# Memory keys, sample attention and the hand-over to the output projection: first weight splits two steps later, the keys' inverse root on GpSimd with later transposes, output-projection weights and the attention mix fetched ahead and split in two column ranges

## The chip, the cores and the metric

The kernel runs on one core of one Trainium2 chip. The metric is the device time of one execution in microseconds (us); lower is better. Times "before" are three timed executions and one profiled execution. The profile was taken on that core.

## What is computed

The reference is one layer of a streaming encoder for a prompt of 1024 rows and a sample of 64 rows that share the weights. Cut to what matters here:

```python
h  = rms_norm(x, g_norm1)
q, k, v, f = split(h @ w_in)                # two kinds of heads, A and B, 8 each, width 64
mix = concat(attend_A(...), attend_B(...))  # 1088 rows (1024 prompt, 64 sample) x 1024
x  = x + mix @ w_o                          # the output projection
kv = rms_norm(mem, g_mem) @ w_mkv           # 256 memory rows, 2048 columns
mk = rms_norm(kv[:, :1024] in 4 heads of 256, g_mk)   # keys;  mv = kv[:, 1024:]
x  = x + mem_attend(rms_norm(x, g_norm2), mk, mv) @ w_mo
x  = x + conv_ffn(rms_norm(x, g_norm3))
```

Every float32 product is made of two parts, "hi" (rounded) and "lo" (what the rounding left), so one product is three matmuls: hi·hi, lo·hi, hi·lo. A **split** is therefore two instructions: a copy on ScalarE that makes hi, and a subtraction on VectorE or GpSimd that makes lo.

## The kernel before, in words

The program is one long straight run of instructions. The code states the work in an order, and a planner then fixes the order of each engine's queue from dependencies and its own estimate of durations; at run time each queue is strictly in order. The stages are: the input projection with prompt attention woven in; the memory keys and values, woven with the attention of the 64 sample rows; the output projection; memory attention; the feed-forward part. All DMAs are issued from the queue of SyncE (SP), also in order.

The change lies between the end of prompt attention and the start of the output projection.

**End of prompt attention** (helpers at L460 to L566). For a head, two score groups are multiplied into one PSUM pair "S" (L499), GpSimd adds the forget bias into a row buffer `s` (L485, L486), VectorE takes the row maximum (L502), ScalarE the exponential (L504), ScalarE or GpSimd scales (L509, L507), TensorE transposes 128x128 blocks into `PT` (L539), which are split (L540, L541) and multiplied with the values into `O` (L554). ScalarE copies half of `O` (`otmp`, L563), VectorE adds the halves (`mix`, L564), SP stores the result to DRAM (`mixd`).

**Memory stage.** L876 to L881 load the memory's first weights and input, split the input (`mhi`, `mlo`, L265 and L266) and, with `split_wm(0, 0)` and `split_wm(0, 1)`, half of the first weights (`mwhi`, `mwlo`, L668 and L669). Then the last four steps of prompt attention follow (`LEFT`, L882); fifteen memory pieces are woven into the last of them. There are 16 **units** (n, t): eight column blocks n of 256, of which n = 0 to 3 are keys and 4 to 7 values, times two row tiles t. A unit is 4 pieces of 6 matmuls into a bank of `pj` (L679); `pj` has two banks, so a unit takes the bank of the unit two before it. `mem_end` finishes a unit. For a key ScalarE squares and sums (`sq`, L695), VectorE adds a constant (L696), `rsq` (L71 to L80) makes the inverse root with a logarithm and an exponential on ScalarE and three small steps on VectorE, and VectorE scales out of the bank (`kv`, L698). `mem_turn` transposes the key on TensorE (L710). It stands in the third piece of the next unit.

**Sample attention.** Eight samples (pairs of heads) go through `load`, `prep`, `splitk`, `score`, `splitv`, `turn`, `sum`, `out` (L717 to L849), each a step behind the other; `PER` says how many memory pieces are woven into each step. Cached keys come through `kraw` buffers, of which there are three. The result goes into `smix`.

**Hand-over.** When no memory piece is left, `open_left` (L962) gives up the memory's SBUF, opens the pool of the projection's streamed weights (`Stream`, L902, splits at L919 and L920), and splits the mix: eight rows k of 1024 columns, each one copy on ScalarE (L979) and one subtraction on VectorE (L980), from `mraw` buffers. In the last step the first of two products is woven in, `first` = output rows m = 0, column ranges 0 and 1; the projection's `ORDER` (L1087) starts with them. L1022 and L1023 add the sample's 64 columns.

## Time and profile before

| what | value |
|---|---|
| median of 3 timed runs | 1781.4 us (1781.03 to 1784.44) |
| profiled execution, its own time | 1788.58 us |
| span of the profile | 1786.6 us |
| TensorE busy | 1717.5 us, 96% of the span |
| VectorE, ScalarE, GpSimd busy | 68%, 53%, 36% |
| prompt attention ends, first memory matmul | 598.69 us |
| last memory matmul starts | 699.47 us |
| first projection matmul on the mix | 710.55 us |

How to read the profile lines: in the timeline each row is a start (us), a duration (us), the engine, the line of the kernel, the operation, and out<-in; "x3" says that three like instructions were merged; the bracket gives the idle time of that engine just before and what ended it. In the table by windows each engine has its busy time and the number of instructions in a stretch; the three last columns are the granted TensorE clock (1.00 is full speed), the busy share of the DMA engines and GB/s. A row of the groups has the count, the busy time in all, and the mean duration in ns. PE is TensorE, DVE VectorE, ACT ScalarE, POOL GpSimd.

### The profile page before, as it was taken

What the parts mean: (1) busy time and instruction counts of PE and PEld (TensorE: products, weight loads), DVE (VectorE), ACT (ScalarE), POOL (GpSimd) and SP (SyncE); (2) the same over time, 40 slices, a digit from 0 to 9 for tenths busy, and PEclk for the clock granted to TensorE, in tenths of its full rate; (3) what the DMA queues carried; (4) which work ended last, traced back from release to release, by engine and by line L of the source; (5) the groups of instructions that cost most, each with busy time, mean ns of one, the idle gap of its engine ahead of it and who ended that gap; (6) DMA issues with size and microseconds to landing.
All of it is one profiled execution on the core that took longest, in us unless ns stands there. A gap on an engine that the chain in (4) does not pass through costs nothing.

```text
span 1786.6 us, 33930 instructions
## 1 busy us (share of the span) xinstructions
PE 1717.5 (96%) x12432; PEld 1668.3 (93%) x12432; DVE 1210.5 (68%) x2643; ACT 941.2 (53%) x2058; POOL 647.3 (36%) x931
## 2 busy tenths in 40 slices
PE   7898999999998898999999999999999999999999
PEld 6888999999997777999999999999999999999999
DVE  5768667677677686433444369877777777649986
ACT  6756667677677577433555456434333333434432
POOL 4556667778777443453443612100000000000000
PEclk8999999999999999999999999999999999999999
DMA  7322222122112777541111563222222222693332
GB/s 251 91 62 64 60 77 78 49 74 76 51 56 83 216 252 219 165 143 56 54 54 60 151 214 104 79 75 77 79 85 85 85 73 73 216 346 130 118 104 88
DMA packets 134391, 199.87 MB, mean 112 GB/s; under 512 B 20984, under 2 KB 74360, under 8 KB 134224
## 3 DMA queue, kind: packets, MB, share of 16 engines
q1 hardware_dynamic: 134224, 197.70, 35.0%
q8 instruction: 98, 1.61, 0.4%
q14 instruction: 69, 0.57, 0.1%
HBM read 155.35 MB, written 45.44 MB: 112 GB/s over the span
## 4 chain that ended last, share of the span: by engine, by line
PE 46%; DVE 4%; issue 2%; ACT 1%; POOL 1%; DMA 1%; SPq 0%; DVEq 0%; ACTq 0%; POOLq 0%
PE W L1449 24%; PE W L1773 11%; PE pj L937 7%; PE S L1192 1%; PE tq L1228 1%; PE O L1228 1%; POOL lo L920 1%; DVE f L1314 0%; PE PT L1215 0%; DMA f<-x2d 0%; DVE lo L920 0%; DMA h<-ad 0%; PE O L1192 0%; ACT hi L1313 0%; DVE qhi L1301 0%
## 5 line engine op out<-in xcount | busy, mean ns | idle before, releaser
L299 PE MATMUL pj<-whi,xhi 128*128 128x384 f32 (+1 forms) x512 | 195.8, 382 | 2.7 <-DVE flog L314 1.6
L299 PE MATMUL pj<-wlo,xhi 128*128 128x384 f32 (+1 forms) x512 | 177.0, 346 | 4.3 <-POOL wlo L123 4.3
L299 PE MATMUL pj<-whi,xlo 128*128 128x384 f32 (+1 forms) x512 | 175.9, 344 | 0.7 <-DVE xlo L131 0.7
L1555 POOL COPY s<-gp 128x2 f32<-128x2 f32 x22 | 15.8, 720 | 335.8 <-DVE gp L1554 335.8
L1449 PE MATMUL W<-h,hi 128*128 128x272 f32 x704 | 134.4, 288 | 1.4 <-ACT qlo L1585 1.4
L504 ACT ACTIVATE s<-s,mx 128x640 f32<-128x640 f32 (+7 forms) x128 | 94.4, 737 | 77.4 <-DVE mx L502 76.5
L1773 PE MATMUL W<-f,hi 128*128 128x272 f32 x672 | 127.1, 287 | 0.1
L541 DVE TENSOR_TENSOR ptl<-PT,pth 128x512 fp32r<-128x512 f32 (+2 forms) x192 | 99.4, 522 | 37.5 <-ACT pth L540 35.3
L1449 PEld LDWEIGHTS W<-h,hi 128*128 128x128 f32 x704 | 110.8, 188 | 1.6 <-ACT qlo L1585 1.6
L540 ACT CAST pth<-PT 128x512 fp32r<-128x512 f32 (+2 forms) x192 | 84.7, 449 | 41.7 <-PE PT L539 39.9
L1773 PEld LDWEIGHTS W<-f,hi 128*128 128x128 f32 x672 | 105.3, 188 | 0.4 <-DVE f L1520 0.4
L299 PEld LDWEIGHTS pj<-wlo,xhi 128*128 128x128 f32 x512 | 99.5, 194 | 5.9 <-POOL wlo L123 5.9
L299 PEld LDWEIGHTS pj<-whi,xhi 128*128 128x128 f32 x512 | 99.4, 194 | 4.3 <-DVE flog L314 1.9
L1449 PE MATMUL W<-h,lo 128*128 128x272 f32 x352 | 101.8, 289 | 0.0
L299 PEld LDWEIGHTS pj<-whi,xlo 128*128 128x128 f32 x512 | 98.3, 192 | 1.4 <-DVE xlo L131 1.2
L1773 PE MATMUL W<-f,lo 128*128 128x272 f32 x336 | 96.7, 288 | 0.0
L539 PE MATMUL PT<-ident,s 128*128 128x128 f32 x528 | 89.9, 277 | 6.9 <-DVE ptl L541 5.4
L1313 ACT CAST hi<-raw 128x512 fp32r<-128x512 f32 x68 | 42.2, 621 | 98.6 <-PE W L1449 59.2
L499 PE MATMUL S<-kh,q 128*128 128x256 f32 (+1 forms) x304 | 77.8, 281 | 13.5 <-DVE mx L502 13.5
L937 PE MATMUL pj<-a,hi 128*128 128x384 f32 (+1 forms) x352 | 89.3, 337 | 0.2 <-DMA mraw<-mixd 0.2
L507 POOL TENSOR_SCALAR s<-s,ssum 128x640 f32<-128x640 f32 (+6 forms) x96 | 70.8, 738 | 47.9 <-DVE ssum L505 34.3
L554 PE MATMUL O<-pth,v 128*128 128x256 f32 (+1 forms) x304 | 76.5, 277 | 8.5 <-DVE mix L564 7.7
(538 smaller groups left out, 6037.6 us busy)
## 6 DMA issues: line engine op xcount, KB each, us to landing
raw<-in_w_down_dram SPq DMA_DIRECT2D x45, 256.0 KB, 2.8
wraw<-in_w_dram SPq DMA_DIRECT2D x56, 192.0 KB, 2.5
raw<-in_w_up_dram SPq DMA_DIRECT2D x41, 256.0 KB, 2.8
h<-ad SPq DMA_DIRECT2D x32, 272.0 KB, 5.5
mwraw<-in_w_mkv_dram SPq DMA_DIRECT2D x16, 512.0 KB, 6.1
raw<-in_w_mo_dram SPq DMA_DIRECT2D x32, 256.0 KB, 3.2
kvraw<-in_w_down_dram SPq DMA_DIRECT2D x32, 256.0 KB, 3.0
ad<-t SPq DMA_DIRECT2D x22, 272.0 KB, 2.2
```

The lines of the kernel that those rows point to most:

```text
L299: pe.matmul(pj[:, :nw], x2[a][:, k, t * P:(t + 1) * P], wt[k][b][:, :nw], start=n == 0, stop=n == 3 * KT - 1)
L499: pe.matmul(sp[:, a:a + (k1 - k0) * P], q, kk[:, h, src], start=m == 0, stop=m == 1)
L504: act.activation(s[:, :n], s[:, :n], ACT.Exp, bias=mx, scale=-1.0, accum_out=sm)
L507: pool.tensor_scalar(s[:, :n], s[:, :n], sm, 1.0, op0=ALU.mult, op1=ALU.mult)
L539: pe.transpose(pt[:, b - ch[0]], self.s[j][:, (b - w0) * P:(b - w0 + 1) * P], ident)
L540: act.copy(hi[:, f:f + n, j], pt[:, f:f + n])
L541: dve.tensor_tensor(lo[:, f:f + n, j], pt[:, f:f + n], f32(hi[:, f:f + n, j]), op=ALU.subtract)
L554: pe.matmul(op[:, cols], groups[p, b // 2].v[:, b % 2, h].rearrange("p a d -> p (a d)"), pt[:, x, cols], start=b == self.full[0] and m == ...
L937: pe.matmul(out()[:, :cn], w[a][:, k % 4], x[b][k][:, c0:c0 + cn], start=k == 0 and n == 0, stop=k == KT - 1 and n == 2)
L1313: act.copy(hi, t)
L1449: pe.matmul(w[:, z, :Q], a(p, j), rights[j][b][:, z * Q:z * Q + Q], start=fresh and begin and j == 0 and x == 0, stop=final and end and j ...
L1773: pe.matmul(ws[m][:, z, :Q], la[p][:, m * P:(m + 1) * P], ra[b][:, z * Q:z * Q + Q], start=first and y == 0 and what in opening, stop=fina ...
```

## The change

Four things are edited.

1. `split_wm(0, 0)` and `split_wm(0, 1)` stand two steps of prompt attention later.
2. A key's constant and inverse root are two GpSimd instructions (an add, and a power of -0.5 with `mhalf`) in place of one VectorE step, two ScalarE steps and three VectorE steps. The key's transpose stands in the second piece of the unit after the next, and `kv` has three buffers in place of two.
3. The pool of the streamed weights and of `x0` lies beneath the memory's pool, so it is open from the start of the stage: the first loads are stated at sample step 4, the first four splits at steps 5 and 6. The first six mix rows are loaded at steps 4 to 6, the last two in `open_left`, all into buffers of the samples' pool: five `mraw`, and the `kraw` buffers, which the samples' keys also use. `sqd` has one buffer in place of two.
4. The mix is split in two column ranges, 0 to 384 and 384 to 1024, in 16 pieces; the first two products are both of column range 0 (m = 0 and m = 1), and `ORDER` starts with these.

```diff
-STAGE, MIXES = 4, 8
+MIXES = 8
+MIXED = {4: ("mraw",) * 2, 5: ("mraw",) * 2, 6: ("mraw", "kraw")}
+WEIGHTS = 5
...
-    left = ExitStack()
+    left, late_left = ExitStack(), ExitStack()
+    wr = late_left.enter_context(tc.tile_pool(name="wr", bufs=1, side="left"))
+    early_x = late_left.enter_context(tc.tile_pool(name="x0", bufs=1, side="left")).tile([P, 384], F32, name="x0")
...
-            dve.tensor_scalar(ms, ms, emem[:, t:t + 1], None, op0=ALU.add)
-            rsq(mp, ms, r, 1)
+            pool.tensor_scalar(ms, ms, emem[:, t:t + 1], 1.0, op0=ALU.add, op1=ALU.mult)
+            pool.tensor_tensor(r, ms, mhalf[:, 0:1], op=ALU.pow)
...
-                if c == 2 and u:
-                    mem_turn(*units[u - 1])
+                if c == 1 and u > 1:
+                    mem_turn(*units[u - 2])
...
-    split_wm(0, 0)
-    split_wm(0, 1)
-    for n in LEFT:
+    for x, n in enumerate(LEFT):
+        if x == 2:
+            split_wm(0, 0)
+            split_wm(0, 1)
         step(n, substeps())
...
-    first = [Product(2 * m, mixr, c, c == 2) for m, c in ((0, 0), (0, 1))]
+    first = [Product(2 * m, mixr, c, c == 2) for m, c in ((0, 0), (1, 0))]
...
+        def split_mix(k, c):
+            hi, lo = (mixr[z][k][:, c] for z in range(2))
+            act.copy(hi, mraws[k][:, c])
+            dve.tensor_tensor(lo, mraws[k][:, c], f32(hi), op=ALU.subtract)
+
+        for k in range(6, KT):
+            load_mix("kraw")
+
+        return ha, [lambda k=k, c=c: split_mix(k, c) for c in (slice(0, first_), rest_) for k in range(KT)]
...
+        for tag in MIXED.get(x, ()):
+            load_mix(tag)
+        if x == WEIGHTS - 1:
+            stream.fetch()
+            nc.sync.dma_start(early_x, i["xT"][0, :, 0:384])
...
+        if WEIGHTS <= x < WEIGHTS + 2:
+            subs += [lambda n=n: stream.upto(n) for n in (2 * (x - WEIGHTS) + 1, 2 * (x - WEIGHTS) + 2)]
```

What the planner makes of it is seen in the queues. All five are the same before and after up to the end of prompt attention and again from the third product of the projection on.

**ScalarE, at the end of prompt attention.** Before, two splits of the memory's weights (`mwhi`) stand ahead of the copy of `O` (`otmp`):

```order
L265 ACTIVATE mhi<-s,gcol 128x256 x3
L668 CAST mwhi<-mwraw 128x512 x2
L563 COPY otmp<-O 64x256
L540 CAST pth<-PT 128x4x128 x2
L668 CAST mwhi<-mwraw 128x512 x2
L265 ACTIVATE mhi<-s,gcol 128x256 x4
L504 ACTIVATE s,ssum<-s,mx 128x896
L540 CAST pth<-PT 128x128
L509 ACTIVATE s<-s,ssum 128x896
L540 CAST pth<-PT 128x2x128
L504 ACTIVATE s,ssum<-s,mx 128x1024
```

Now the same stretch reads (`hi<-raw` is a split of the projection's first streamed weights):

```order
L267 ACTIVATE mhi<-s,gcol 128x256 x3
L565 COPY otmp<-O 64x256
L542 CAST pth<-PT 128x4x128 x2
L672 CAST mwhi<-mwraw 128x512 x2
L542 CAST pth<-PT 128x128
L672 CAST mwhi<-mwraw 128x512
L542 CAST pth<-PT 128x2x128
L267 ACTIVATE mhi<-s,gcol 128x256 x4
L506 ACTIVATE s,ssum<-s,mx 128x896
L565 COPY otmp<-O 64x256
L672 CAST mwhi<-mwraw 128x512
L929 CAST hi<-raw 128x512
```

The copy of `O` stands ahead of the weights, and two of the weights' copies have gone behind the next exponential. All four of the projection's stated first splits have come up to the end of prompt attention: the first is the last row shown, the others stand up to 14 rows later, two of them behind the last exponential.

**GpSimd, at the first two key units.** Before, between the last scaled scores and the first sample's small steps (`s<-s,stok` is the sample's forget bias, `mwlo` the low part of a memory weight):

```order
L762 TENSOR_SCALAR s<-s,stok 128x1088
L669 TENSOR_TENSOR mwlo<-mwraw,mwhi 128x512
L892 MEMSET sq_9094 128x128
L892 MEMSET sq_9095 128x128
L765 AFFINE_SELECT s<-s 64x64 x2
```

Now, with the roots (`mms` is the squared sum, `mr` the inverse root) of the first and the second unit:

```order
L700 TENSOR_SCALAR mms<-mms,emem 128x1
L701 TENSOR_TENSOR mr<-mms,mhalf 128x1
L766 TENSOR_SCALAR s<-s,stok 128x1088
L673 TENSOR_TENSOR mwlo<-mwraw,mwhi 128x512
L896 MEMSET sq_9077 128x128
L896 MEMSET sq_9078 128x128
L769 AFFINE_SELECT s<-s 64x64 x2
L673 TENSOR_TENSOR mwlo<-mwraw,mwhi 128x512
L700 TENSOR_SCALAR mms<-mms,emem 128x1
L701 TENSOR_TENSOR mr<-mms,mhalf 128x1
```

The second unit's root stands behind a sample's bias, two weight splits and four small steps.

**TensorE, at the hand-over.** Before, from the end of the seventh sample's sum (`su` is a sample's finished result, `s` its weights, `a` the mix):

```order
L835 MATMUL O<-svh,ptl 128x256
L847 MATMUL PT<-ident,su 64x128
L822 MATMUL PT<-ident,s 128x128 x4
L822 MATMUL PT<-ident,s 64x128
L937 MATMUL pj<-a_10467,hi 128x384
```

Now, from the last rows of the eighth sample's sum (`vc` and `svh` are the high parts of cached and new values):

```order
L839 MATMUL O<-vc,ptl 128x256
L839 MATMUL O<-svh,pth 128x256
L839 MATMUL O<-svh,ptl 128x256
L949 MATMUL pj<-a_10458,hi 128x384 x2
L949 MATMUL pj<-a_10466,hi 128x384
```

The first product on the mix stood ahead of the eighth sample's sum and now stands behind it. Between the last memory matmul and this product the queue also holds the seventh sample's transposes and sum and the eighth's queries and scores, with no memory matmul among them.

More of the change, by code (lines that the diff above doesn't have):

```diff
@@ L725, in load @@
             p, n = self.p, self.ctx + S
-            self.qd = mq.tile([S, 4, P], F32, name="sqd", bufs=2)
+            self.qd = mq.tile([S, 4, P], F32, name="sqd", bufs=1)
             nc.sync.dma_start(self.qd.rearrange("t h d -> t (h d)"), sqk[p])
@@ L869, in hybrid_step @@
             line.append(piece)
-    line.append(lambda: mem_turn(*units[-1]))
     def step(n, subs):
@@ L892, in hybrid_step, with load_mix @@
         pool.memset(f32(zq[x][:, 1:3]), 0.0)
+    mraws = []
+    def load_mix(tag="mraw"):
+        k = len(mraws)
+        mraws.append(mq.tile([P, T], F32, name=tag, bufs={"mraw": 5, "kraw": 3}[tag]))
+        nc.sync.dma_start(mraws[k], mixd[k])
     samples = [Sample(p) for p in SAMPLES]
@@ L928, in done @@
             self.upto(j + 5)
+    stream = Stream(wr)
     def gemm(out, j, x, chunk, end):
@@ L962, in open_left @@
     def open_left():
[L963 removed]
         left.close()
[L965 to L967 removed]
         ha = mixes.enter_context(tc.tile_pool(name="ha", bufs=1, side="left"))
[L969 removed]
         mixr.extend(parts(ha, "a"))
[L971 to L990 removed]
+        first_, rest_ = CHUNKS[0][1], slice(CHUNKS[0][1], T)
+        def split_mix(k, c):
[5 more added lines that the diff above has]
+        return ha, [lambda k=k, c=c: split_mix(k, c) for c in (slice(0, first_), rest_) for k in range(KT)]
     old, mixes_todo, ha = [], [], None
@@ L1008, in hybrid_step @@
         del line[:PER[x]]
-        if ha and not mixes_todo:
-            stream.upto(4)
-            if todo:
-                main = todo.pop(0).pieces
+        if WEIGHTS <= x < WEIGHTS + 2:
+            subs += [lambda n=n: stream.upto(n) for n in (2 * (x - WEIGHTS) + 1, 2 * (x - WEIGHTS) + 2)]
+        if ha and len(mixes_todo) <= KT:
+            main = todo.pop(0).pieces
         subs += mixes_todo[:MIXES]
@@ L1085, in project @@
                 deferred.append((4, lambda c=c: after(c, acc[c])))
-    ORDER = [(0, 0), (0, 1), (1, 0), (0, 2), (1, 1), (1, 2)] + [(m, c) for m in range(2, 8) for c in range(3)]
+    ORDER = [(0, 0), (1, 0), (0, 1), (0, 2), (1, 1), (1, 2)] + [(m, c) for m in range(2, 8) for c in range(3)]
     e2 = hb.tile([P, 9], F32, name="e2")
```

27 lines of the change are left out of this document (3 added, 24 removed).

## The prediction

> **What bounds the kernel now.** I read the head of the page, then the busy times and the granted clock in windows around the change, then TensorE's waits, then the timeline.
>
> ```profile
> span 1786.6 us, 33930 instructions
> PE 1717.5 (96%) x12432; PEld 1668.3 (93%) x12432; DVE 1210.5 (68%) x2643; ACT 941.2 (53%) x2058; POOL 647.3 (36%) x931
> ```
>
> TensorE is busy for 96% of the span, so an edit can only win what TensorE idles, or runs at a reduced clock, where the change acts.
>
> ```profile
> 574.00:575.00 1.00, 0.00 (x0) 0.00 (x0) 0.00 (x0) 0.69 (x2) 1.00 (x4) 0.50 1.00 384
> 584.00:585.00 1.00, 0.67 (x5) 0.46 (x4) 1.00 (x1) 0.12 (x1) 0.93 (x2) 0.91 1.03 418
> 707.00:708.00 1.00, 0.00 (x0) 0.00 (x0) 0.91 (x1) 0.95 (x3) 0.00 (x0) 0.53 0.94 303
> 717.00:718.00 1.00, 1.00 (x8) 1.00 (x8) 1.00 (x3) 1.00 (x2) 0.00 (x0) 0.85 0.79 260
> 725.00:735.00 10.00, 10.00 (x63) 10.00 (x62) 3.26 (x6) 5.15 (x10) 4.72 (x4) 1.00 0.62 183
> ```
>
> The columns are the stretch, then PE, PEld, DVE, ACT, POOL busy, then the granted clock. The queues agree up to the end of prompt attention and again from the third projection product, and from 725 TensorE has no gap. So everything is decided between 571 and 725. In it lie two windows at half clock, of some 10 us each (574 to 584, 707 to 717), each begun in a gap of TensorE, and between them small waits:
>
> ```profile
> PE PT L710 <- DVE kv L698: 3.5, 4, 1.3
> PE pj L679 <- POOL mwlo L669: 2.0, 3, 1.0
> ```
>
> These are TensorE's two largest waits from 598 to 701 (total us, times, longest): the key that must be transposed, and the low part of a memory weight.
>
> **A. The weights' splits two steps later.**
>
> ```profile
> 574.31 1.14 ACT L668 CAST mwhi<-mwraw 128x512 fp32r<-128x512 f32 x2 [1.24 <-DMA mwraw<-in_w_mkv_dram]
> ...
> 575.47 0.37 ACT L563 COPY otmp<-O 64x256 f32<-64x256 f32 x1
> ...
> 575.48 3.00 DVE L669 TENSOR_TENSOR mwlo<-mwraw,mwhi 128x512 fp32r<-128x512 f32 x1 [1.89 <-ACT mwhi L668]
> ...
> 575.69 1.01 POOL L485 TENSOR_SCALAR s<-bias,ctok 128x896 f32<-128x896 f32 x1
> ...
> 577.89 0.74 POOL L486 TENSOR_SCALAR_AFFINE_SELECT s<-s 128x128 f32<-128x128 f32 x1
> ...
> 578.51 0.42 DVE L564 TENSOR_TENSOR mix<-O,otmp 64x256 f32<-64x256 f32 x1
> ...
> 578.85 1.07 DVE L502 CUSTOM_DVE_ANT_0 s<-S,s 128x896 f32<-128x896 f32 x1
> ...
> 579.07 0.55 PE L554 MATMUL O<-pth,v 128*128 128x256 f32 x1 [7.69 <-DVE mix L564]
> ...
> 598.69 0.28 PE L679 MATMUL pj<-mwhi,mhi 128*128 128x256 f32 x1
> ```
>
> TensorE stands 7.69 us for `mix`, which stands behind the subtraction of 3.00, and its `otmp` behind two copies that waited for a DMA. With the splits later, `otmp` follows the `mhi` rows that end at 573.06 (574.31 − 1.24), `mix` comes at about 573.6, and TensorE restarts near 574.1, 5.0 earlier. All of that does not come through. The next link is the first row maximum (578.85). It needs GpSimd's bias, which ends at 576.70 (575.69 + 1.01), and its selection, up to 0.74 more, so it can start near 577.1, 1.7 earlier; the four maxima then follow each other through one pair of banks. ScalarE also gets the four stream splits here, at 0.57 each (half of 1.14), two behind the last exponential. I take +1.6 for the gain at the first memory matmul (598.69 to about 597.0), between 0 (the stream splits eat it) and 5.0.
>
> **B. The root on GpSimd, the transpose a unit later, first four keys.**
>
> ```profile
> 602.69 0.39 ACT L695 ACTIVATE sq<-pj 128x256 f32<-128x256 f32 x1 [1.82 <-PE pj L679]
> ...
> 606.05 0.48 DVE L698 SCALAR_TENSOR_TENSOR kv<-pj,mr,gmk 128x256 f32<-128x256 f32 x1
> ...
> 606.68 0.41 PE L710 MATMUL PT<-ident,kv 128*128 128x128 f32 x2 [1.27 <-DVE kv L698]
> ...
> 610.98 0.41 PE L710 MATMUL PT<-ident,kv 128*128 128x128 f32 x2 [1.01 <-DVE kv L698]
> ...
> 615.34 0.41 PE L710 MATMUL PT<-ident,kv 128*128 128x128 f32 x2 [0.86 <-DVE kv L698]
> ...
> 724.23 0.51 PE L937 MATMUL pj<-a,hi 128*128 128x384 f32 x2
> ...
> 724.76 0.51 PE L937 MATMUL PT<-a,hi 128*128 128x384 f32 x2
> ```
>
> The nearest rows for the new instructions are GpSimd's groups in the prompt's norms (four columns where the new ones have one; the mean ns of one is behind the comma):
>
> ```profile
> L250 POOL TENSOR_TENSOR r<-m,mhalf 128x4 f32<-128x4 f32 x32 | 32.7, 1021 | 31.0 <-DVE m L249 30.2
> ...
> L244 POOL TENSOR_SCALAR m<-m,eps 128x4 f32<-128x4 f32 x32 | 9.3, 290 | 60.2 <-DVE m L241 60.2
> ```
>
> From `sq` to the end of `kv` is now 3.84 (602.69 to 606.53). The new chain is `sq` 0.39 and its read-out 0.2, the add 0.29, the power 1.02, `kv` 0.48, with handoffs about 2.7. The transpose a unit later has a whole unit in hand: 24 matmuls of 256 columns, by the three of 384 columns in 0.53 (724.23 to 724.76) 0.177 × 2/3 = 0.12 each, 2.9. So the 3.5 of key waits go. What is late next is the bank: with two banks of `pj`, unit u + 2 waits for `kv` of unit u, and GpSimd's queue decides that.
>
> ```profile
> 601.29 1.18 POOL L762 TENSOR_SCALAR s<-s,stok 128x1088 f32<-128x1088 f32 x1 [0.52 <-DMA s<-negs]
> ...
> 604.24 1.30 POOL L669 TENSOR_TENSOR mwlo<-mwraw,mwhi 128x512 fp32r<-128x512 f32 x1 [1.77 <-ACT mwhi L668]
> ...
> 605.47 0.36 POOL L892 MEMSET sq<- 128x128 f32 x2
> ...
> 605.77 0.54 POOL L765 TENSOR_SCALAR_AFFINE_SELECT s<-s 64x64 f32<-64x64 f32 x2
> ...
> 606.39 1.28 POOL L669 TENSOR_TENSOR mwlo<-mwraw,mwhi 128x512 fp32r<-128x512 f32 x1
> ```
>
> The second unit's root stands behind these: 1.18 + 1.30 + 0.36 + 0.54 + 1.28 = 4.66 us of work, queued behind the first root. From the first unit's end 0.6 for `sq`, 1.31 for the first root, 4.66, 1.31 for the second and 0.48 for `kv` make 8.4, some 8.9 with handoffs. The fourth unit, which needs that bank, could start after two units and two pairs of transposes, 2 × 2.9 + 0.4 to 0.7 = 6.2 to 6.5: a new wait of about 2.4. So of the first three waits (1.27 + 1.01 + 0.86 = 3.1) 2.4 is given back: +0.7, between −1.7 (one more such wait) and +3.1 (none).
>
> For the roots that go off VectorE this row bears a warning:
>
> ```profile
> L669 DVE TENSOR_TENSOR mwlo<-mwraw,mwhi x16: 679/814/2997, 575.5 to 688.3; 128x512 fp32r<-128x512 f32 x16
> ```
>
> One and the same subtraction takes 0.68 to 3.00 on VectorE; 3.00 is the one that had GpSimd's bias, at 575.69, beside it. The Trainium skill, "SBUF — State Buffer", section "Who interferes with whom", says that a VectorE instruction with two SBUF inputs and a GpSimd instruction that reads SBUF shut each other out. That rule speaks against moving work to GpSimd. What the mechanism would cost here is worked out from rows as rival 5.
>
> **C. The rest of the memory stage.**
>
> ```profile
> 622.13 0.50 PE L797 MATMUL S<-kchi,sq 128*128 128x512 f32 x1 [0.88 <-ACT kchi L774]
> ```
>
> The first score of a sample waited 0.88 for its keys' high part; the key loads stood behind stores of `kv` in SP's queue. With earlier stores it goes, and so does the fourth key wait (3.5 − 3.1 = 0.4): +1.2. The 2.0 for `mwlo` stay or grow, since GpSimd gets 1.31 more per key unit; the bounds are −2 (as much again) and +3.3 (0.9, 0.4 and 2.0 all gone). One `sqd` buffer costs nothing so long as its transposes stand ahead of the next load's arrival.
>
> **D. The hand-over.**
>
> ```profile
> 698.44 0.40 PE L754 MATMUL tq<-ident,sqd 64*128 64x64 f32 x4
> ...
> 699.47 0.28 PE L679 MATMUL pj<-mwhi,mlo 128*128 128x256 f32 x1
> ...
> 704.48 0.28 PE L835 MATMUL O<-svh,ptl 64*128 64x256 f32 x1
> ...
> 705.73 0.19 ACT L808 ACTIVATION_READ_ACCUMULATOR s<-s,mx 128x1 f32 x1
> ...
> 708.78 0.39 PE L847 MATMUL PT<-ident,su 128*64 128x128 f32 x1 [4.03 <-DVE su L843]
> ```
>
> Now the last memory matmul ends at 699.75 and the third product starts at 724.76: 25.0, with a wait of 4.03 and the half clock in it. Afterwards no product stands between the samples: 5.0 to finish the seventh sample's sum (699.75 to 704.76), the eighth from its query to its exponential 7.5 (698.44 to 705.92), its transposes, the split of its weights (0.57, as in A) and its sum (10 × 0.12) 2.6 with handoffs; then 48 matmuls of 384 columns at 0.177, 8.5. 5.0 + 7.5 + 2.6 + 8.5 = 23.6, so the gain is about +1.5 if the clock stays full; the splits of the mix lie beside the samples. Here TensorE works thinly for some 15 us, though with no wait as long as 4.03. Where the clock drops for 10 us, half of the work in them is lost, 5.0 if they are full and 2.4 if they lie half in waits: 26 to 28.5, or −1 to −3.5. The bounds are −3.5 and +2.5 (the seventh's end lies a little beside the eighth's start).
>
> The rows show half clock at 574.00, at most 2.6 us after that gap began (579.07 − 7.69 = 571.38), and at 707, at most 3.2 after the other began (708.78 − 4.03 = 704.75); it came back some 10 us later. The Trainium skill, "TensorE: Matmul & The Clock Gate", Part 1, gives a half rate after an idle window of about 3.4 us. By that rule a drain of shorter gaps keeps the clock and the sum stands; by the trace's earlier fall it might not, which is rival 1. [...]
>
> **Sum.** 1.6 + 0.7 + 1.2 + 1.5 = +5.0. The profiled execution took 1788.58 (its span 1786.6, the rest lies around it), 7 above the median of the runs; the terms are differences of one stage, so I subtract them from both: 1783.6 profiled, 1776.4 for the median of 1781.4.
>
> **Rivals.**
> 1. *The half clock comes back at the hand-over.* D turns to −1 to −3.5, and the sum to 0 to 2.5: about 1780. For it: two such windows in this very stretch, and a thin drain. Against: no single gap as long as 4.03.
> 2. *The gap at the end of prompt attention comes through whole.* A is 5.0, B 3.1: 5.0 + 3.1 + 1.2 + 1.5 = 10.8, so 1770.6. For it: 7.69 is one wait. Against: the row maxima and their bias bind next.
> 3. *Slower: GpSimd's queue holds the banks.* Per key unit GpSimd gets 1.31 of root beside 1.30 of weight split, 2.6 of the unit's 2.9, and each sample adds its bias (1.18), selections and `vc`. If four more units wait 2.4 each, 5.0 − 9.6 = −4.6: 1786.0; if all seven, 1793. It decides when GpSimd is behind by more than a unit, 2.9, on average, which the 4.66 above shows for one unit only.
> 4. *The change moves loads but not what binds.* The mix's early loads and the streamed splits (which wait for a DMA, and on ScalarE stand ahead of exponentials) take from A what they gave to D, and the drain goes on as before: +1 to +3, within what can be told from no change. For it: the splits of the mix still need the eighth sample's place in the queues.
> 5. *VectorE and GpSimd get in each other's way.* If each of the eight roots keeps VectorE from its own work for its whole 1.31, 8 × 1.31 = 10.5 of VectorE's time is gone where VectorE has little to give:
>
> ```profile
> 640.00:650.00 10.00, 9.63 (x71) 8.48 (x70) 9.30 (x25) 8.01 (x20) 3.44 (x4) 1.00 0.76 248
> ```
>
>    VectorE is busy for 9.30 of 10 there. 5.0 − 10.5 = −5.5: 1786.9. This is the mechanism of the page on SBUF named above. Against it: the root's operands are one column each, and most subtractions took 0.7 to 0.8.
>
> **How the numbers follow.** About 0.2% (3.6 us) is what a measurement of this kernel can tell from no change. The forecast case (gain 3.6 to 9, 1772.4 to 1777.8) has 0.45; rival 1 0.20, rival 2 0.10, rival 3 0.09, rival 5 0.03, rival 4 0.13. Faster by over 0.2%: 0.45 + 0.10 = 0.55; within 0.2%: 0.20 + 0.13 = 0.33; slower: 0.09 + 0.03 = 0.12. The range takes in rival 2's price with some 2 us more of A's bound below, and above rivals 1 and 4 and the start of rival 3: 1768.5 to 1784.0.
>
> **What the profile after would show.** Right: `otmp` ahead of `mwhi` and TensorE back near 574 instead of 579.07; the first memory matmul near 597; no wait of the transposes for `kv`, and one wait of `pj` for `kv`, near 2.4, in the fourth unit; the last memory matmul to the third product 23.5; full clock at the hand-over; nothing moved after it but the offset. Wrong: `pj` waiting for `kv` in more units (rival 3), a granted clock of 0.5 in the drain or the first two products (rival 1), or a wait of 4 to 5 us for a streamed weight or a mix row there, which no term has.

## The result, and the profile after

The changed kernel takes 1797.47 us (median of five, 1794.71 to 1803.79) against 1781.4 us (five runs, 1780.52 to 1784.44): ratio 1.0088, 95% interval [1.0066, 1.0110]. It is slower by 0.9%, where the forecast was 0.3% faster; the time lies above the whole range. The head of the page after:

```profile
span 1795.7 us, 33913 instructions
PE 1722.1 (96%) x12432; PEld 1672.8 (93%) x12432; DVE 1202.1 (67%) x2619; ACT 939.6 (52%) x2050; POOL 650.3 (36%) x947
```

TensorE's 12432 instructions are the same, and its busy time is 4.6 us longer. Matmuls that take longer are the first sign of a slower clock. The table by windows, cut at the four stages (from the last matmul of the input projection to the first on the memory; to the last on the memory; to the third projection product; to the last projection matmul), shows where. Columns as in the prediction: PE, PEld, DVE, ACT, POOL busy, then the granted clock. Before:

```profile
559.90:598.70 38.80, 26.09 (x176) 22.58 (x175) 29.42 (x64) 29.12 (x61) 22.26 (x31) 0.87 0.61 191
598.70:699.80 101.10, 92.11 (x657) 80.83 (x655) 71.75 (x178) 65.32 (x167) 43.33 (x43) 1.00 0.71 225
699.80:724.80 25.00, 19.73 (x90) 16.61 (x91) 18.11 (x37) 18.07 (x41) 8.60 (x5) 0.80 0.62 197
724.80:814.80 90.00, 89.15 (x541) 88.07 (x540) 30.55 (x52) 33.25 (x64) 43.12 (x38) 1.00 0.47 149
```

After:

```profile
557.00:597.60 40.60, 29.46 (x175) 25.96 (x174) 30.85 (x62) 30.88 (x65) 26.37 (x33) 0.78 0.55 171
597.60:701.60 104.00, 93.91 (x652) 83.52 (x651) 62.62 (x141) 62.10 (x147) 49.88 (x61) 0.97 0.76 240
701.60:729.50 27.90, 21.37 (x93) 17.74 (x94) 15.56 (x39) 16.83 (x41) 1.79 (x2) 0.76 0.34 114
729.50:825.30 95.80, 92.10 (x542) 90.83 (x541) 32.81 (x65) 34.76 (x73) 43.02 (x38) 0.96 0.45 140
```

All four stages are longer, by 1.8, 2.9, 2.9 and 5.8: 13.4 us in one execution. (The two spans lie only 9.1 apart, because the profiled execution before was 7 above its median; 2.9 of the difference lies in its input projection, 559.9 against 557.0 at its end.) Stretch less PE busy is what TensorE idled: 27.8 before, 31.5 after, 3.7 more. The clock's part is worked out in windows of half a microsecond: PE busy times (1 − granted clock), summed over a stage, is the work that was not done there. It gives 2.1, 0.0, 3.8 and 0.0 us before, and 6.3, 3.0, 5.5 and 3.0 after, so 11.8 more. (11.8 and 3.7 exceed 13.4: where slow work fills what would else have been a wait, nothing is lost, so the clock's sum is an upper bound.) **In these two profiles most of the loss is half clock, the rest waits.** TensorE's waits between 560 and 760 after (total, times, longest):

```profile
PE S L501 <- DVE mx L504: 5.2, 4, 2.1
PE O L556 <- ACT pth L542: 4.4, 2, 3.2
PE PT L851 <- DVE su L847: 3.7, 4, 1.5
PE pj L949 <- DVE qhi L1076: 2.8, 1, 2.8
...
PE S L801 <- ACT kchi L778: 2.7, 3, 1.5
PE pj L683 <- DVE kv L702: 2.0, 1, 2.0
...
PE pj L683 <- POOL mwlo L673: 1.5, 2, 1.0
```

The 7.69 for `mix` and the 3.5 for the key's transpose are gone, as meant; a wait of 3.2 for `pth` is what is left in place of the 7.69. In their place stand the row maxima (`mx`, 5.2 in four pieces), the one bank wait that the prediction named (2.0; it said 2.4), and a wait of 2.8 for `qhi` at L949, in the seventh product of the projection, where the prediction had nothing moving.

The hand-over after, in windows of 1 us:

```profile
702.00:703.00 1.00, 0.30 (x1) 0.11 (x1) 0.14 (x1) 0.94 (x4) 0.00 (x0) 1.00 0.96 252
...
704.00:705.00 1.00, 0.35 (x1) 0.19 (x1) 0.54 (x1) 0.58 (x2) 0.00 (x0) 1.00 0.83 257
...
707.00:708.00 1.00, 0.00 (x0) 0.00 (x0) 0.86 (x3) 0.88 (x4) 0.00 (x0) 1.00 0.81 295
708.00:709.00 1.00, 0.56 (x4) 0.43 (x4) 0.40 (x2) 0.64 (x4) 0.00 (x0) 1.00 0.47 177
709.00:710.00 1.00, 0.69 (x4) 0.49 (x3) 0.63 (x3) 1.00 (x3) 0.00 (x0) 0.80 0.20 76
710.00:711.00 1.00, 1.00 (x3) 0.55 (x3) 0.89 (x2) 0.61 (x2) 0.31 (x1) 0.50 0.01 2
...
722.00:723.00 1.00, 1.00 (x5) 1.00 (x5) 0.93 (x2) 0.54 (x2) 0.00 (x0) 0.50 0.00 0
723.00:724.00 1.00, 1.00 (x7) 1.00 (x6) 0.87 (x2) 0.00 (x0) 0.00 (x0) 0.88 0.00 0
```

The clock halves at 709.6 and is back at 723.2: a share of 0.80 is full speed for 0.6 of a window and half speed for the rest, and 0.88 is half speed for its first 0.24. The first projection products, from 719, run with TensorE fully busy at half speed.

### The profile page after: what moved, and what is told of

Same layout as the page of the kernel before. It is cut to its first block, busy times and chain, and to the rows that moved or that the text cites. A ratio compares the mean times of both kernels' runs of the same rounds, so it can differ in the third digit from the quotient of the medians.

```text
span 1795.7 us, 33913 instructions
## 1 busy us (share of the span) xinstructions
PE 1722.1 (96%) x12432; PEld 1672.8 (93%) x12432; DVE 1202.1 (67%) x2619; ACT 939.6 (52%) x2050; POOL 650.3 (36%) x947
## 4 chain that ended last, share of the span: by engine, by line
PE 51%; DVE 1%; POOL 1%; issue 1%; ACT 0%; DVEq 0%; POOLq 0%; ACTq 0%
PE W L1452 25%; PE W L1776 13%; PE pj L949 7%; PE W L949 2%; PE S L1195 1%; PE tq L1231 1%; PE O L1231 1%; POOL lo L930 1%; PE PT L1218 0%; PE O L1195 0%; PE PT L1176 0%; POOL s L1210 0%; DVE f L1317 0%; ACT hi L929 0%; DVE qhi L1304 0%
## 5 line engine op out<-in xcount | busy, mean ns | idle before, releaser
L1776 PEld LDWEIGHTS W<-f,hi 128*128 128x128 f32 x672 | 105.3, 188 | 0.0
L949 PE MATMUL pj<-a,hi 128*128 128x384 f32 (+1 forms) x352 | 90.5, 341 | 2.8 <-DVE qhi L1076 2.8
```

Source lines behind the costliest of these rows:

```text
L949: pe.matmul(out()[:, :cn], w[a][:, k % 4], x[b][k][:, c0:c0 + cn], start=k == 0 and n == 0, stop=k == KT - 1 and n == 2)
L1776: pe.matmul(ws[m][:, z, :Q], la[p][:, m * P:(m + 1) * P], ra[b][:, z * Q:z * Q + Q], start=first and y == 0 and what in opening, stop=fina ...
```

## The experiments

Three theories stand against each other. **The clock**: the change makes TensorE's work from the last samples to the projection thinner, and TensorE runs at half clock there and again at the seventh product. **The root**: on GpSimd it costs by itself, through the order of the queues. **The splits**: moved behind the gap, they cost more there than the gap was worth. All ratios are against the kernel before, in five rounds, with a 95% interval; the name in brackets is that of the run. "Tail" is the end of prompt attention, the first of the four stages above. No experiment leaves out a part of the computation. A stage time is that of one profiled execution. In the input projection, whose queues no edit touches, the clock's sum came to 2.2 to 8.9 in the twenty profiles, so a difference of a few us in one stage of two profiles proves little alone.

**One part at a time.** Three pieces of the change were tried apart. The later splits, "S":

```diff
-    split_wm(0, 0)
-    split_wm(0, 1)
-    for n in LEFT:
+    for x, n in enumerate(LEFT):
+        if x == 2:
+            split_wm(0, 0)
+            split_wm(0, 1)
```

The root, "R":

```diff
-            dve.tensor_scalar(ms, ms, emem[:, t:t + 1], None, op0=ALU.add)
-            rsq(mp, ms, r, 1)
+            pool.tensor_scalar(ms, ms, emem[:, t:t + 1], 1.0, op0=ALU.add, op1=ALU.mult)
+            pool.tensor_tensor(r, ms, mhalf[:, 0:1], op=ALU.pow)
```

The later transpose ("turn"), "T":

```diff
-        kv = mp.tile([P, 256], F32, name="kv", bufs=2)
+        kv = mp.tile([P, 256], F32, name="kv", bufs=3)
...
-                if c == 2 and u:
-                    mem_turn(*units[u - 1])
+                if c == 1 and u > 1:
+                    mem_turn(*units[u - 2])
```

Before with S (e1):

> Before, with the first weight splits two steps later and nothing else. Clock theory (the changed queues put TensorE into more gaps, each of which brings some 10 us of half clock; the moved splits stand ahead of the row maxima on VectorE): the wait of 7.69 for the mix goes, waits of 1 to 2 us for the maxima come, the half clock lasts longer, and the end is 1 to 5 us later, 1782 to 1786. GpSimd theory (the loss comes from the inverse roots on GpSimd): no root is moved here, so the gain of term A of the prediction shows, 1.6 us, 1780.

Measured: 1.0034 [1.0022, 1.0047]; slower, where the GpSimd theory expected a gain, and by more than the clock theory's 5 us. In its profile the tail is no longer than before (38.5, for 38.8); the memory stage takes 103.1 for 101.1, the projection 94.1 for 90.0.

Before with R and T (e2):

> Before, with the inverse root on GpSimd, the transpose a unit later and three key buffers, nothing else. Clock theory: the key waits of 3.5 us go, one new wait of about 2 us for the bank comes, 1 to 3 us faster, 1778 to 1780. GpSimd theory: slower by most of the measured loss, 1788 to 1797.

Measured: 1.0042 [1.0030, 1.0054].

After without S (e3):

> The changed kernel with the first weight splits back in their old place. Clock theory: the tail loses the new waits for the maxima and the half clock at the first memory units, 2 to 6 us faster than the changed kernel, 1791 to 1795; the hand-over stays slow. GpSimd theory: as the changed kernel or slower, 1797 to 1800.

Measured: 1.0071 [1.0059, 1.0083].

After without R and T (e4):

> The changed kernel with root, transpose and key buffers as they were before. Clock theory: within 3 us of the changed kernel, 1795 to 1800, with the loss still at the end of prompt attention and from the hand-over on. GpSimd theory: most of the loss goes, 1781 to 1787.

Measured: 1.0045 [1.0031, 1.0059]. R with T costs 0.42% alone and 0.43% in company (1.0088 − 1.0045), so it is not the whole. S costs 0.34% alone; its 0.17% in company (1.0088 − 1.0071) lies within the intervals and is not shown. Neither theory's expectation for e4 was met: it came out between them.

Before with R alone (e5):

> Before, with the inverse root of the keys on GpSimd (two instructions) and nothing else; the transpose stays in its old place. Root theory (the two roots' place in GpSimd's queue makes the banks and the low parts of the weights late): 4 to 9 us slower than before, the loss in the memory stage. Transpose theory (the loss of the last pair of edits comes from the transpose a unit later): within 2 us of before.

Measured: 1.0033 [1.0022, 1.0045].

Before with T alone (e6):

> Before, with the transpose a unit later and three key buffers, the root as it was. Root theory: the key waits of 3.5 us go and nothing is late instead, 1 to 4 us faster than before. Transpose theory: 4 to 9 us slower than before.

Measured: 1.0005 [0.9997, 1.0014]. So the price is R's: the later transposes change nothing in the whole that can be told, the root on GpSimd costs 0.33%. That is the theory of the root, and it goes against the forecast's +0.7 for B. The place was expected in the memory stage; e5's one profile, of an execution 2 us under its median, doesn't show it there (101.6, for 101.1). And the 1 to 4 us expected of T did not come, though its profile has them where they were meant: the memory stage takes 99.0 for 101.1. The projection gives them back: 93.6 for 90.0, with a wait of 1.80 for `qhi` ahead of the seventh product and 1.7 lost to the clock, though T touches nothing there.

**The clock.** After (e7), with 50 transposes of the identity that nobody reads, put into the waits of the last two samples and the seventh product, so that TensorE is busy there; the other queues are unchanged (shortened):

```diff
+    def keep(out, n, prev):       # on TensorE, in order behind prev
+        for _ in range(n):
+            pe.transpose(out, ident, ident)
+    keep(pt[:, 0], 4, ...)        # seventh sample's weights; 4 before its sum, 8 before su
+    keep(pt[:, 0], 11, ...)       # eighth's; 4 before its sum
+    keep(bank("PT")[:, :P], 19, ...)   # ahead of the seventh product
```

> The changed kernel with 50 transposes of the identity that nobody reads in TensorE's queue: 4, 4, 8, 11 and 4 in the five waits between the last memory matmul and the first product on the mix, 19 in the wait ahead of the seventh product; every other queue is as it was. Clock theory: the granted clock stays at 1.00 from the last memory matmul on, the 5.5 and 3.0 us lost at half clock there go, and it is 5 to 9 us faster than the changed kernel though it does more. Wait theory (the loss is the waits themselves): the same time as the changed kernel, or up to 2 us more.

Measured: 1.0048 [1.0036, 1.0060], against 1.0088 without them. Its stage rows, hand-over and projection:

```profile
702.70:726.60 23.90, 20.47 (x125) 17.44 (x126) 15.31 (x39) 16.81 (x41) 1.79 (x2) 1.00 0.38 128
726.60:819.30 92.70, 91.53 (x560) 90.12 (x559) 34.65 (x65) 34.28 (x73) 43.45 (x38) 1.00 0.46 144
```

The clock is 1.00 in both (0.76 and 0.96 in after), the hand-over is 4.0 shorter and the projection 3.1. Work that does nothing made the kernel 7 us faster; the waits were filled, not taken away. So some 0.4% of the 0.9% goes when TensorE is kept busy in these two places.

For the hand-over that is the theory of the clock, and it was found again: in four later kernels with the same fills (e9, e11, e12, e17) it takes 23.6 to 23.9 at a clock of 1.00. The projection's gain was not found again. In the same four it takes 94.4 to 95.5, at a clock of 1.00 too. The rows of e17:

```profile
696.40:720.00 23.60, 20.46 (x125) 17.41 (x126) 15.71 (x37) 17.66 (x47) 1.83 (x2) 1.00 0.39 133
720.00:814.40 94.40, 91.37 (x559) 90.13 (x559) 32.09 (x64) 33.75 (x67) 43.02 (x38) 1.00 0.46 142
```

There TensorE stands longer near the end of the projection, 1.5 to 2.4 for `kSh` (the sum of squares that GpSimd adds up for the next norm), where e7 and after have 0.2. So the hand-over's 4 us, 0.2%, are shown to be half clock; that the 3 us of the seventh product are, only e7 and e16 below say.

Before, filled in its two large gaps in the same manner (e8: 32 transposes in the 7.69, 24 in the 4.03):

> The kernel before with 32 such transposes in its wait of 7.69 us at the end of prompt attention and 24 in its wait of 4.03 us at the hand-over; a few rows of the first two products also change places. Clock theory: the half clock at the hand-over (3.8 us lost) goes and the one at the end of prompt attention (2.1) goes or gets shorter: 2 to 6 us faster than before. Wait theory: within 1.5 us of before.

Measured: 1.0008 [0.9999, 1.0016]. The hand-over went from 25.0 to 22.5 at full clock, the output projection from 90.0 to 91.8, with a wait of 1.63 for `qhi`: there a part of what was won ahead of the projection was lost in it. The clock theory's 2 to 6 us did not come; as a whole, this is what the wait theory expected. So a clock that is kept is not by itself a gain.

After, filled as in e7 and in four waits of the tail (e9: 16, 10, 8 and 3 more):

> The changed kernel with the 50 transposes of e7 and 37 more in four waits at the end of prompt attention (16, 10, 8, 3); every real instruction stands where it stands in the changed kernel. Clock theory: the half clock at the end of prompt attention and in the first memory units (5.8 and 2 us lost) goes as well: 3 to 7 us faster than e7, that is 1785 to 1789 where before takes 1784. Wait theory: as e7, 1791 to 1794.

Measured: 1.0054 [1.0039, 1.0068]. The tail is 1.8 shorter than after's (38.8 against 40.6) but the whole gains nothing over the fills of the hand-over alone: the projection took 95.5 again, the memory stage 105.3. What was won ahead of the memory stage is not seen at the end. This expectation failed.

**The root's place in GpSimd's queue.** After (e10), with the sample's bias, its selections and two memsets behind the second unit's root (shortened):

```diff
+            if (n, t) == (0, 1): root.append(last_pool())
...
+                if SAMPLES.index(p) >= 2: behind.append(last_pool())   # sample bias
...
+    for ins in behind: tc.add_manual_dep(ins, root[0].name, ...)       # order only
```

> The changed kernel with a sample's bias and its selections and two memsets moved behind the second unit's root in GpSimd's queue; no other queue changes. Queue theory (the root waits for its turn, as term B of the prediction has it): the wait of 2.0 us of the fourth unit goes or falls under 0.6, and with it at times a half clock: 1.5 to 5 us faster than the changed kernel. Contention theory (a root on GpSimd costs by keeping VectorE from its work): within 1 us of the changed kernel.

Measured: 1.0062 [1.0048, 1.0075]; the wait of 2.0 is gone, and the ratio is 0.26% lower, though the interval still touches that of 1.0088.

After with R undone and all fills (e11):

> e9 with the inverse root back on ScalarE and VectorE; the later transpose and the three key buffers stay. If the root on GpSimd costs by itself what e5 showed (0.33%, 6 us), this is 4 to 7 us faster than e9, at 1779 to 1784, level with before or faster. If the root's cost was only the half clock behind its waits, and that is luck of the moment: 0 to 3 us faster than e9.

Measured: 1.0015 [1.0005, 1.0025], 0.39% under the same kernel with the root on GpSimd (1.0054).

After with all fills and the second root first (e12):

> e9 with e10's order on GpSimd. By the queue theory the two gains add: 1.5 to 5 us faster than e9, 1781 to 1787. By the contention theory: as e9.

Measured: 1.0037 [1.0024, 1.0050], 0.17% under 1.0054; these two intervals overlap as well. Taken as they stand, 0.17 of 0.39, or 0.26 of 0.43, was the root's place behind the bias; twice the same way makes it likely, not shown. What the rest is, the next two asked. VectorE's waits from 598 to 702 after have one line that the profile before has nothing like:

```profile
DVE kv L702 <- POOL mr L701: 14.1, 8, 4.2
```

VectorE stands 14.1 us at the head of its queue for eight roots. If that is the price, taking VectorE out of it must win (e13; one line left out):

```diff
-            dve.scalar_tensor_tensor(kv, pj, r, gmk, op0=ALU.mult, op1=ALU.mult)
+            act.copy(cp, pj)
+            pool.tensor_scalar(cp, cp, r, 1.0, op0=ALU.mult, op1=ALU.mult)
+            pool.tensor_tensor(kv, cp, gmk, op=ALU.mult)
```

> The changed kernel, but ScalarE copies a key unit out of its bank right behind the squares, and GpSimd scales it behind the root (two instructions), so that VectorE has no part in it and no engine waits for GpSimd's root. VectorE-queue theory (what the root costs is that VectorE's queue stands at the scaling, 14.1 us in all, for the root): 4 to 7 us faster than the changed kernel, as in e4. Contention theory (work on GpSimd slows VectorE): GpSimd has more work, so as the changed kernel or up to 5 us slower.

Measured, in after: 1.0110 [1.0093, 1.0127].

> Before with root and scaling on GpSimd in the way of e13, the transpose in its old place. VectorE-queue theory: the 6 us that e5 lost go, within 2 us of before. Contention theory: 6 us or more above before.

Measured (e14), in before with R: 1.0061 [1.0048, 1.0073]. Both are slower. TensorE's waits in the memory stage and the hand-over of the first of the two:

```profile
PE pj L683 <- POOL mwlo L673: 6.0, 5, 3.1
...
PE PT L717 <- POOL kv L705: 1.7, 2, 1.4
```

More work on GpSimd makes its other products late: the low parts of the memory weights, 1.5 in after, now hold TensorE for 6.0. So that VectorE's standing is the price was not confirmed: this test moved the stall onto another engine, and doesn't tell how much of the price it was. Both times the contention theory's expectation was met, as e10's was not. The traces speak against it: the VectorE instructions of the memory stage that a kernel with the root on GpSimd shares with its partner took 0.3 us less in all in e9 than in e11, and 0.7 more in e18 than in e17 (two kernels further down), far from a price of 6 us.

**The rows of the projection.** After (e16), with the last sample's transpose some 16 matmuls earlier on TensorE, ahead of the second product (shortened):

```diff
+            marks["out"] = last_pe()                                # transpose of su
...
+                if j == 2 and c0 == 0 and k + n == 0 and x is mixr:
+                    fillers.append((last_pe(), marks["out"].name))  # order only
```

> The changed kernel with the last sample's transpose ahead of the second product in TensorE's queue (some 16 rows earlier). Row theory (the seventh product waits because the rows of x are loaded into memory that the samples give up only when the mix's last columns are split, and these stand behind that transpose): the wait of 2.85 us of the seventh product falls under 1 and the half clock behind it goes, 3 to 6 us faster than the changed kernel. Rival (the rows' loads are late for the queue of SyncE or the DMAs themselves): within 1 us.

Measured: 1.0062 [1.0049, 1.0075]. The projection took 92.4 in place of 95.8, at full clock; its wait for `qhi` is still 2.2. So of the 3.4 only 0.6 is the wait, and 3.0 is the half clock behind it, which didn't come this time. The row theory's wait under 1 didn't come either, so the gain is not its own; and the interval touches that of 1.0088.

**Sums.** e13, e16 and all fills together (e15):

> e13, e16 and the 87 transposes of e9 in one kernel. If root, half clock and row loads are what the change costs, they add up: within 3 us of before, 1781 to 1787. If something else has a part, it stays 5 us or more above before.

Measured: 1.0085 [1.0069, 1.0100]. Tail, hand-over and projection were mended (39.0, 25.0, 93.7), the memory stage took 113.4 because of the scaling on GpSimd; it couldn't answer the question. So, without that edit, e11 with the earlier transpose (e17):

> Changed kernel with the root back on ScalarE and VectorE, idle transposes in the waits (as in e11) and the last sample's transpose ahead of the second product (as in e16). e11 stood at 1.0015 of before, its last part at 95.3 from the third product to the end of the output projection, 3.6 of it idle. Theory that the x rows come late because the mix's last splits do: the waits for qhi (0.7) and kSh (2.0) go in part, that part falls to 92 to 94, the ratio to 0.9995 to 1.0010. Theory that the loads themselves are what is late: nothing moves, ratio 1.0015, part 95.3.

Measured: 1.0023 [1.0014, 1.0032]. And e12 with it (e18):

> Changed kernel with the root still on GpSimd but the second unit's ahead of the sample bias (as in e10), idle transposes in the waits (as in e12), and the last sample's transpose ahead of the second product (as in e16). e12 stood at 1.0037. If the parts add: 1.0037 less 0.1 to 0.2%, so 1.0017 to 1.0027, and what is left over e17 is the price of the root on GpSimd apart from its place behind the bias, 0.2%. If the place in the queue was the whole price of the root: within 0.1% of e17.

Measured: 1.0054 [1.0041, 1.0068]. Both are above what either theory expected. With the fills, the earlier transpose wins nothing (1.0015 to 1.0023, 1.0037 to 1.0054). That would fit a gain by the clock alone in e16, but the fills did not keep it everywhere: e18's projection took 96.6 at 0.96. And the root on GpSimd still costs 0.31% over the same kernel without it, though no bank waits for it any more. Their profiles show one place for that. The first score of a cached sample, root on GpSimd and mended:

```profile
612.19 0.77 PE L831 MATMUL S<-kchi,sq 128*128 128x512 f32 x1 [1.84 <-ACT kchi L808]
```

ScalarE's `kchi` stood 2.32 for its keys there (`kraw`), until 611.48. SP had issued their load behind the store of a transposed key:

```profile
607.51 0.37 SPq L745 DMA_DIRECT2D kmd<-kt  x1
607.93 0.46 SPq L772 DMA_DIRECT2D kraw<-in_cbk_dram  x1
```

Its clock after the wait:

```profile
612.00:616.00 4.00, 3.81 (x14) 3.45 (x15) 2.30 (x5) 2.07 (x7) 1.14 (x2) 0.50 1.01 341
```

The same sample in e11, with all fills and the root on ScalarE and VectorE, waits 0.17 and keeps the clock; its wait and its window:

```profile
615.52 0.50 PE L823 MATMUL S<-kchi,sq 128*128 128x512 f32 x1 [0.17 <-ACT kchi L800]
```

```profile
612.00:616.00 4.00, 3.83 (x29) 3.35 (x28) 3.49 (x12) 2.65 (x8) 0.64 (x2) 1.00 0.96 310
```

With the root on GpSimd and no bank wait, TensorE came for that score 14.6 us after the first memory matmul (612.19 − 1.84 − 595.8), against 18.7 (615.52 − 0.17 − 596.7). The load was not late: it went 12.1 after that matmul, where e11's went 13.7 after it (610.38 − 596.7). But TensorE was earlier by more, the keys were not there, and the wait was followed by half speed. Over the memory stage TensorE idles 7.7 here and 8.1 there, but loses 4.8 to the clock, against 1.6. So in these two profiles the longer stage (103.0, for 99.8) is the clock, behind a wait that an earlier TensorE ran into.

## Why the prediction was wrong

The steps that failed are the price of the root as one bank wait (B), the hand-over at full clock (D), and the stage after it, which was to be moved only (the last step below). The gain of A was lost on the way as well, where the row maxima did not follow each other.

**A, the tail.** The mechanism held up to its last step. TensorE came back, now for `pth` and no more for `mix`, at 571.62, which is 14.6 after the end of the input projection where it was 19.2 (579.07 − 559.9): 4.6 earlier, for the 5.0 predicted. The first row maximum:

```profile
574.09 1.09 DVE L504 CUSTOM_DVE_ANT_0 s<-S,s 128x896 f32<-128x896 f32 x1 [1.69 <-POOL s L488]
...
575.64 3.03 DVE L268 SCALAR_TENSOR_TENSOR mlo<-s,gcol,mhi 128x256 fp32r<-128x256 f32 x4
578.60 1.21 DVE L504 CUSTOM_DVE_ANT_0 s<-S,s 128x1024 f32<-128x1024 f32 x1
...
580.38 3.35 DVE L673 TENSOR_TENSOR mwlo<-mwraw,mwhi 128x512 fp32r<-128x512 f32 x2
583.65 1.08 DVE L504 CUSTOM_DVE_ANT_0 s<-S,s 128x896 f32<-128x896 f32 x1
```

It came 17.1 after that end where it had come 18.95: 1.9 earlier, for 1.7. The step that failed is "the four maxima then follow each other": the four subtractions for `mlo` (1.66 before, 3.03 here) and two for `mwlo` (3.35) stand between them on VectorE, and TensorE waits 1.09, 1.80 and 2.08 for them. The prediction moved the work out of one gap and didn't ask into which one it went. The Trainium skill, "SBUF — State Buffer", section "Who interferes with whom", fits: these subtractions took 1.66 in before, and 3.03 here beside GpSimd's biases; the prediction had the warning row (0.68 to 3.00) and used it for a rival only. And the half clock, which ended at 584 before, lasted to 590 here: 6.3 lost for 2.1. That is no chance of one execution: in the seven profiles with S and an unfilled tail the idle time is 9.0 to 11.8 and the clock's sum 5.8 to 7.3, in the six without S 11.8 to 12.7 and 2.0 to 5.1. So A's 1.8 on the wrong side is 1.6 of idle time won and some 4 of clock lost. The prediction had no term for the clock in A at all. Filling the gaps did not pay here: e9's tail of 38.8 gave no time back.

**B, the first keys.** The new wait was right in place, cause and size (2.0 at the fourth unit, for 2.4), and the root was cheaper than its bound (0.26 + 0.56 on GpSimd, for 1.31). But the sum of waits wasn't the price: R costs 0.31 to 0.43% in five pairs of kernels (in two of them with T), some 6 to 8 us, the wait 2.0. In four of these pairs the time goes in the memory stage, 105.3 in e9 for 99.8 in e11, 103.0 in e18 for 99.5 in e17, 104.0 in after for 101.1 in e4, 107.9 in e2 for 101.1 in before; in e5's profile it doesn't show. What was missed is that three other queues stand behind GpSimd's chain: VectorE at `kv`, SP at the key's store, and behind that store the next keys' load. Which of them makes the price is not shown. Rival 3 had the engine right and the path wrong: it priced banks, only one of which waited.

**C, the rest of the stage.** "With earlier stores it goes": the wait for the keys' high part rose instead, from 0.88 to 2.4 in two scores of that stage. The loads of the keys, which were to come with the earlier stores, were not earlier against TensorE's work:

```profile
612.17 0.46 SPq L744 DMA_DIRECT2D kraw<-in_cbk_dram  x1
...
614.20 0.42 SPq L744 DMA_DIRECT2D kraw<-in_cbk_dram  x1
```

612.17 is 14.6 after the stage's first matmul; before, the same load went at 612.82, 14.1 after it. The store ahead of it needs the second key, whose root stood behind the sample's bias. That is not the whole of it: with that root first (e10) the load went 13.7 after the stage's first matmul, and the keys' high part still cost 2.8 in two scores.

**D, the hand-over.** The sum was right and the clock wasn't. Seventh sample's end, predicted 5.0: 5.1. Query to exponential, 7.5: 7.3. The rest at half speed. With the clock kept by idle transposes the stage is 23.9, for 23.6. In after it is 27.9, in the 26 to 28.5 of **rival 1**, which had 0.20 and is what happened in this stage; its whole, about 1780, is not. "Against: no single gap as long as 4.03" was the wrong argument. The longest gap ahead of the fall is this:

```profile
708.20 0.27 PE L851 MATMUL PT<-ident,su 128*64 128x128 f32 x1 [1.22 <-DVE su L847]
```

The windows from 702 to 709 hold 0.00 to 0.98 of busy time. The rule of the Trainium skill, "TensorE: Matmul & The Clock Gate", Part 1, that an idle window of some 3.4 us halves the rate, doesn't account for this fall: no such window is here. Nor does a fall end by itself: before, the 10 us of half clock ended at 717.3, after the first 3.4 us in which TensorE had no pause (1.55, 2.69 and 3.41 busy in the three stretches of 3.4 from 707.07 on).

**"Nothing moved after it but the offset."** This step, outside all the terms, was the largest single miss: 5.8 in the last stage. The seventh product after:

```profile
747.28 0.56 DVE L1076 TENSOR_TENSOR qhi<-pj,qhi 128x384 f32<-128x384 f32 x1 [0.48 <-DMA qhi<-in_xT_dram]
...
747.98 0.98 PE L949 MATMUL pj<-a,hi 128*128 128x384 f32 x2 [2.85 <-DVE qhi L1076]
```

It needs the bank of the fifth, which waits for a row of x. The queues' order is unchanged there, and so was read as unchanged time. The first product's row is loaded ahead; SP's first load of the others came at 733.09, 3.6 after the third product's start (729.53), where before:

```profile
724.83 0.33 SPq L1074 DMA_DIRECT2D x1d<-qhi  x1
725.21 0.42 SPq L1066 DMA_DIRECT2D qhi<-in_xT_dram  x1
```

it came at 0.45 (725.21 − 724.76). Before, the row loads ran level with the third product, and the long hand-over paid for them. The new order of products and splits is not needed for the wait: e1, e6 and e8, which have before's order of products, wait 1.8, 1.8 and 1.6 at the same place. Their hand-overs are shorter than before's by 0.5 to 2.5, so TensorE comes sooner to the rows; how much of after's 2.85 is the new order is not shown. The half clock after the wait took 3.0 more in after.

**Sum.** Two causes are shown by experiments: half clock at the hand-over, some 0.2%, and the root on GpSimd, 0.31 to 0.43%, the latter as the price of an edit and not by its path. Half clock behind the seventh product's wait was up to 0.2% more. With the root back and the fills in, 0.15 to 0.23% stay (1.0015 and 1.0023, the same queues but for the last sample's transpose). By their profiles this rest lies in the projection: the other three stages together are 2.4 and 2.9 shorter than before's, the projection is 5.3 and 4.4 longer at full clock. 2.2 of that is the 19 idle transposes in the wait for the row, 2 to 3 more is waiting, the most of it for `kSh`. Why that comes late is open. Open is also how much of the root's price runs through VectorE's 14.1 and how much through SP's loads; the one test of the former made GpSimd later by as much. No version beat the kernel before.

## What to carry to other kernels

Before you count a removed wait as won, ask where TensorE's work then lies thin: several waits of at most 1.2 us cost the clock here as one of 4.0 did, and the products behind them pay, not the waits. A queue whose order is unchanged can still become the bound when what stands ahead of it on another engine gets shorter; so follow the loads (here the rows of x and the cached keys) against the engine that uses them, not against the clock on the wall. And when work goes to a free engine, list who stands at the head of a queue for its result: here the engine was busy for a third of the span, the moved root took 0.8 us, and it still cost 0.3%.

## What the runs showed of the hardware

The granted clock fell to 0.50 after some 8 us in which TensorE was busy by about a half and idle for at most 1.22 at a time, and came back 14 us later, when it had been busy without a break for some 7. The same wait doesn't always do it: the wait of 2.2 for `qhi` left the clock at 1.00 in one profile, and 2.85 at the same place halved it for nearly 7 us. Such falls come and go from one execution to the next: the changed kernel's five executions, spread over 9.1 us (3.9 before), had mean granted clocks of 0.986, 0.988, 0.985, 0.981 and 0.979, from the fastest to the slowest. Transposes of the identity in the waits held the clock at the hand-over in seven of the eight kernels that had them; their own time stands where the wait was. On GpSimd, an add on 128x1 took 0.26 and the power 0.56, where the groups of four columns had 0.29 and 1.02: the power's time goes with its columns more than the add's does.
